# Passages between sublayers: five products ahead of the norm and three with it, squares added on VectorE, G units packed toward the middle of a stage

## Chip, core and metric

The kernel runs on one core of a Trainium2 chip. The metric is the device time of one execution in microseconds (us); of several runs the median counts.

## The reference, cut to what matters

Two transformer blocks run over T = 256 tokens of width D = 1024, all in fp32. The change touches the six sublayers of the first block; the second block (short convolution, two expert layers, differential attention) is untouched.

```python
def rmsnorm(x, g):
    y = x * lax.rsqrt(jnp.mean(x * x, axis=-1, keepdims=True) + EPS)
    return y * g

def swiglu(h, w_gu, w_down):                 # w_gu: 1024 x 5632, w_down: 2816 x 1024
    gate, up = jnp.split(h @ w_gu, 2, axis=-1)
    return (jax.nn.silu(gate) * up) @ w_down

def sublayer(x, shift, scale, gate, g_pre, g_post, fn, res_weight):
    h = rmsnorm(x, g_pre) * (1 + scale[:, None, :]) + shift[:, None, :]
    return x + res_weight * gate[:, None, :] * rmsnorm(fn(h), g_post)
...
mods = jnp.split(c_act @ cond_w[layer] + cond_b[layer], 9, axis=-1)   # shift, scale, gate of each sublayer
```

Each of the two layers runs three sublayers: an FFN (`swiglu`), a mixer (GLA, gated linear attention, in the first layer; MLA, latent attention, in the second) and another FFN.

## The kernel before

**Weights.** Every fp32 product is three matmuls in a reduced form of fp32 (hi x hi, hi x lo, lo x hi; lines 297 to 299, and 320 to 323 in the passages). So each weight passes through a split. It comes as a unit of 128 x 1024 (512 KB): SP issues its DMA into a raw buffer, ACT casts it to the high half (L237), DVE subtracts for the low half (L248). The products of the conditioning vector `c` with `cond_w` and the like are not matmuls: such a "G unit" is one DVE instruction over a raw buffer (L251), which the profile shows with a second row that reads the sum out. `build_plan` writes one list of all units, W and G, and its `mix` deals a stage's G units evenly between the W units that follow the first `LEAD`. Raw buffers are a ring of four, with one or two more during an FFN; there are eight slots for split pairs. `next_w` is called where a weight is used: it splits everything up to that weight, then `prefetch(n_ahead)` splits up to three units more, if their slots are free.

**Order.** Each engine runs its instructions in the order of the code. A DVE instruction that is written behind a split cannot start before that split, and a split not before its DMA and its cast.

**An FFN.** 22 row blocks f. For each, the `gu` product gives the gate and the up part in one bank; ACT takes SiLU (L677), DVE multiplies (L678), ACT casts the product to its high half (L345), DVE subtracts for its low half `tL` (L348; called `a` for the first 14). `out_proj` then multiplies by `w_down` into `y`, which needs all 22. As each `y` block ends, ACT squares it (L557) and DVE adds the squares (L560); `pst` sums them over the channels on PE.

**A passage.** Between two sublayers PE would stand still while x is updated and its norm taken. So the first products of the next sublayer are computed before its norm is known: `ahead` updates x block by block (L604, L607), scales it (L471, L462), multiplies it by the weights of four output blocks (`first`, 258 columns wide for two extra terms), and sums x's squares with eight products `st` (L351). `scaled_rstd` takes the root on ACT and the reciprocal on DVE (L622 to L625), `apply` normalises x (L434, L435, L428) for four more products (`second`), and the `first` products are scaled afterwards (`late`). x stays scaled by an unknown factor `x_r`; the next update multiplies by it (L599), and before the convolution `unscale` (L614) divides it out, during the last FFN. There are five such passages: to GLA, to the second FFN, to the third FFN (with the products of MLA's keys and values, "kv"), to MLA, and to the fourth FFN.

In time, the four FFNs lie at about 55 to 225, 376 to 571, 572 to 784 and 888 to 1085 us, GLA and MLA between them.

## Time and profile before

| | |
|---|---|
| median of 3 runs | 2981.62 us (2979.09 to 2990.97) |
| profiled execution | 2977.33 us, span 2975.4 us |
| mean granted clock of TensorE | 0.985 of full speed |
| PE, DVE, ACT busy | 95%, 81%, 49% of the span |
| DMA | 630.43 MB, mean 212 GB/s |

The engines are PE (TensorE, matmuls), PEld (its weight loads), DVE (VectorE), ACT (ScalarE), POOL and SP (which issues the DMAs). "L248" is line 248 of the kernel. `out<-in` names the tiles written and read. A row of a timeline has start, duration, engine, line, operation, tiles and shapes; what stands in brackets at its end is how long its engine sat idle before it and which instruction ended that. A row of the waits says which engine and line waited for which, the total, the number and the longest. PEclk is the granted clock of TensorE, 1.00 for 2.4 GHz and 0.50 for 1.2.

### The profile page before, as it was taken

What the parts mean: (1) busy time and instruction counts of PE and PEld (TensorE: products, weight loads), DVE (VectorE), ACT (ScalarE), POOL (GpSimd) and SP (SyncE); (2) the same over time, 40 slices, a digit from 0 to 9 for tenths busy, and PEclk for the clock granted to TensorE, in tenths of its full rate; (3) what the DMA queues carried; (4) which work ended last, traced back from release to release, by engine and by line L of the source; (5) the groups of instructions that cost most, each with busy time, mean ns of one, the idle gap of its engine ahead of it and who ended that gap; (6) DMA issues with size and microseconds to landing.
All of it is one profiled execution on the core that took longest, in us unless ns stands there. A gap on an engine that the chain in (4) does not pass through costs nothing.

```text
span 2975.4 us, 60705 instructions
## 1 busy us (share of the span) xinstructions
PE 2831.2 (95%) x24914; PEld 2764.5 (93%) x24914; DVE 2399.3 (81%) x4373; ACT 1465.7 (49%) x2140; POOL 6.8 (0%) x16
## 2 busy tenths in 40 slices
PE   6998999999999999999999999989799999999998
PEld 5997889999879999999999999988799999999998
DVE  6978689687768978998997887767689988788754
ACT  4555555455555545545444444446554544444543
POOL 0000000000000000000000000000000000000000
PEclk8999999999999999999999999999999999999999
DMA  7995569578636966465556557874245655655662
GB/s 270 360 327 181 185 225 335 203 282 302 213 128 247 335 211 229 144 190 178 178 193 221 176 178 250 300 254 142 98 131 187 190 172 190 215 177 177 221 191 93
DMA packets 173174, 630.43 MB, mean 212 GB/s; under 512 B 19319, under 2 KB 20343, under 8 KB 172768
## 3 DMA queue, kind: packets, MB, share of 16 engines
q1 hardware_dynamic: 172080, 623.98, 62.8%
q8 instruction: 195, 3.19, 0.4%
q0 software_dynamic: 816, 2.57, 0.3%
q14 instruction: 83, 0.68, 0.1%
HBM read 625.43 MB, written 1.05 MB: 211 GB/s over the span
## 4 chain that ended last, share of the span: by engine, by line
PE 71%; DVE 12%; DMA 10%; ACT 5%; issue 2%; SPq 0%; ACTq 0%; DVEq 0%
PE u L297 7%; PE u L299 7%; PE u L298 7%; PE ya L297 6%; PE ya L298 6%; PE ya L299 6%; PE gu L299 3%; PE gu L298 3%; PE gu L297 3%; DVE xl L248 2%; DMA raw<-in_peer_v_dram 2%; PE y L298 2%; PE y L299 2%; PE y L297 2%; DVE wl L248 2%
## 5 line engine op out<-in xcount | busy, mean ns | idle before, releaser
L237 ACT CAST wh<-raw 128x1024 fp32r<-128x1024 f32 x535 | 559.7, 1048 | 573.5 <-PE ya L298 228.4
L248 DVE TENSOR_TENSOR wl<-raw,wh 128x1024 fp32r<-128x1024 f32 x535 | 653.2, 1224 | 165.4 <-ACT wh L237 163.1
L297 PE MATMUL u<-hH,wh 128*128 128x256 f32 x2048 | 575.3, 281 | 0.0
L299 PE MATMUL u<-hH,wl 128*128 128x256 f32 x2048 | 570.1, 278 | 2.0 <-DVE wl L248 1.9
L298 PE MATMUL u<-hL,wh 128*128 128x256 f32 x2048 | 569.1, 278 | 0.0
L298 PE MATMUL ya<-hL,wh 128*128 128x256 f32 x1424 | 395.3, 278 | 8.3 <-DVE hL L348 8.3
L297 PE MATMUL ya<-hH,wh 128*128 128x256 f32 x1424 | 400.0, 281 | 2.6 <-ACT hH L345 2.6
L299 PE MATMUL ya<-hH,wl 128*128 128x256 f32 x1424 | 394.4, 277 | 0.0
L299 PEld LDWEIGHTS u<-hH,wl 128*128 128x128 f32 x2048 | 386.7, 189 | 3.5 <-DVE wl L248 3.1
L298 PEld LDWEIGHTS u<-hL,wh 128*128 128x128 f32 x2048 | 385.6, 188 | 0.0
L297 PEld LDWEIGHTS u<-hH,wh 128*128 128x128 f32 x2048 | 384.6, 188 | 0.0
L248 DVE TENSOR_TENSOR xl<-raw,xh 128x1024 fp32r<-128x1024 f32 x235 | 286.1, 1222 | 94.9 <-ACT xh L237 93.8
L237 ACT CAST xh<-raw 128x1024 fp32r<-128x1024 f32 x235 | 244.8, 1049 | 237.5 <-DMA raw<-in_ffn_gu_dram 49.4
L298 PEld LDWEIGHTS ya<-hL,wh 128*128 128x128 f32 x1424 | 268.3, 188 | 9.7 <-DVE hL L348 9.7
L297 PEld LDWEIGHTS ya<-hH,wh 128*128 128x128 f32 x1424 | 268.2, 188 | 3.2 <-ACT hH L345 3.2
L299 PEld LDWEIGHTS ya<-hH,wl 128*128 128x128 f32 x1424 | 268.5, 189 | 0.0
L299 PE MATMUL gu<-hH,xl 128*128 128x256 f32 x744 | 208.3, 280 | 4.8 <-DVE xl L248 4.8
L298 PE MATMUL gu<-hL,xh 128*128 128x256 f32 x744 | 208.1, 280 | 0.0
L297 PE MATMUL gu<-hH,xh 128*128 128x256 f32 x744 | 208.0, 280 | 0.0
L298 PE MATMUL ya<-hL,xh 128*128 128x256 f32 x624 | 174.7, 280 | 10.1 <-DVE hL L348 10.0
L297 PE MATMUL ya<-hH,xh 128*128 128x256 f32 x624 | 175.2, 281 | 0.5 <-ACT hH L345 0.4
L299 PE MATMUL ya<-hH,xl 128*128 128x256 f32 x624 | 172.9, 277 | 0.0
(566 smaller groups left out, 7278.6 us busy)
## 6 DMA issues: line engine op xcount, KB each, us to landing
raw<-in_peer_u_dram SPq DMA_DIRECT2D x256, 512.0 KB, 3.7
raw<-in_peer_v_dram SPq DMA_DIRECT2D x234, 512.0 KB, 3.8
raw<-in_ffn_gu_dram SPq DMA_DIRECT2D x107, 512.0 KB, 5.1
raw<-in_cond_w_dram SPq DMA_DIRECT2D x92, 512.0 KB, 4.9
raw<-in_ada_w_dram SPq DMA_DIRECT2D x71, 512.0 KB, 4.6
raw<-in_ffn_down_dram SPq DMA_DIRECT2D x57, 512.0 KB, 5.0
fix<-in_ffn_gu_dram SPq DMA_DIRECT2D x53, 512.0 KB, 5.2
fix<-in_cond_w_dram SPq DMA_DIRECT2D x43, 512.0 KB, 5.1
```

Of the source, the lines that this page charges most:

```text
L237: self.nc.scalar.copy(self.slots[self.slot[n]][0], self.raw[n])
L248: nc.vector.tensor_tensor(wl, raw, wh.bitcast(F32), op=OP.subtract)
L297: mm(out, lhsT=wh, rhs=xh, start=start, stop=False, **kw)
L298: mm(out, lhsT=wh, rhs=xl, start=False, stop=False, **kw)
L299: mm(out, lhsT=wl, rhs=xh, start=False, stop=stop, **kw)
```

## The change

- In the passages to GLA and to the second and fourth FFN, `ahead` takes five products and `apply` three; the passage to the third FFN keeps four and four, that to MLA its three.
- Where there are more than three products ahead, DVE adds the squares of seven blocks one to another as they come, and PE sums two operands in place of eight; the products of k = 5 stand ahead of the sums.
- `scaled_rstd` is called before `prefetch`, which takes two units and not three; the one behind `apply` takes one and not two.
- The reciprocal of `x_r` moves from `apply` into `unscale`, and x is unscaled in every sublayer, block by block between other work.
- In `out_proj`, over the last 24 row blocks, splits run up to five units ahead, and two at the last unit.
- `LEAD` goes from 9 to 11, and with `TAIL` the last five W units of a stage come without G units.

```diff
--- before.py
+++ after.py
@@ -39,12 +39,12 @@
 
 SCRATCH = 8192
 
-AHEAD, AHEAD_MLA, AHEAD_PEER = 3, 2, 2
+AHEAD, AHEAD_END, AHEAD_MLA, AHEAD_PEER = 3, 5, 2, 2
 
 N_START = 6
 
 CUTS = (56, 76, 112, 150, 154, 194, 200, 248, 248)
-LEAD, LEAD_CONV, LEAD_U, LEAD_V, LEAD_ATTN = 9, 24, 100, 74, 12
+LEAD, TAIL, LEAD_CONV, LEAD_U, LEAD_V, LEAD_ATTN = 11, 5, 24, 100, 74, 12
 N_U = 10
 
 
@@ -437,8 +437,7 @@
                 low(d - 1)
         low(KO - 1)
         self.hold = False
-        nc.vector.reciprocal(self.x_r, self.x_r)
-        self.prefetch(2)
+        self.prefetch(1)
 
     def ahead(self, A, S, n):
 
@@ -452,15 +451,19 @@
         s2 = S.unsqueeze(2).to_broadcast([128, KO, 2])
         nc.scalar.copy(tH[:, :, T:T + 2], s2)
         nc.vector.tensor_tensor(tL[:, :, T:T + 2], s2, tH[:, :, T:T + 2].bitcast(F32), op=OP.subtract)
-        outs = [self.bank("y", "first") for _ in range(n)]
+        outs = [self.bank(b, "first") for b in "yyyym"[:n]]
         cols = [o[:, 0:T + 2] for o in outs]
         ws = self.open_group(n)
         st = self.bank("x", "st")[:, :T]
         sq = self.yg
 
+        n_add = KO - 1 if n > 3 else 1
+
         def low(d):
             nc.vector.scalar_tensor_tensor(tL[:, d, 0:T], x[:, d], A[:, d:d + 1], tH[:, d, 0:T].bitcast(F32),
                                            op0=OP.mult, op1=OP.subtract)
+            if 0 < d < n_add:
+                nc.vector.tensor_tensor(sq[:, 0], sq[:, 0], sq[:, d], op=OP.add)
             if d < 5:
                 self.k_mm(cols, ws, ht, d)
 
@@ -475,12 +478,16 @@
             if d:
                 low(d - 1)
         low(KO - 1)
-        for d in range(KO):
-            self.sums(st, sq[:, d], d == 0, d == KO - 1)
-        self.prefetch(3, True)
-        for k in range(5, KO):
+        if n > 3:
+            self.k_mm(cols, ws, ht, 5)
+        self.sums(st, sq[:, 0], True, False)
+        for d in range(n_add, KO):
+            self.sums(st, sq[:, d], False, d == KO - 1)
+        r = self.scaled_rstd(st)
+        self.prefetch(2, True)
+        for k in range(6 if n > 3 else 5, KO):
             self.k_mm(cols, ws, ht, k)
-        return outs, self.scaled_rstd(st)
+        return outs, r
 
     def ahead_ln(self, m, stats, n):
 
@@ -571,8 +578,12 @@
             y = self.bank("m" if lead and d < lead + 2 else "y", "y")[:, :T]
             for k in range(KB):
                 if n % 8 == 0:
-                    self.hold = n + 8 >= KB * (KO - lead)
+                    left = KB * (KO - lead) - n
+                    if left <= 24:
+                        self.n_ahead = AHEAD_END if left > 8 else 2
                     cur = self.next_w()
+                    self.n_ahead = AHEAD
+                    self.hold = left <= 8
                 s = slice(n % 8 * 128, n % 8 * 128 + 128)
                 self.mm3(y, cur[0][:, s], cur[1][:, s], aH[k], aL[k], k == 0, k == KB - 1)
                 n += 1
@@ -592,16 +603,14 @@
     def scaled_update(self):
 
         nc = self.nc
-        q = s = self.t("rstd")
+        s = self.t("rstd")
         nc.scalar.activation(s, self.post_st, AF.Sqrt, scale=1.0 / D, bias=self.cst(C_E6))
-        if self.x_scaled:
-            q = self.t("rstd")
-            nc.vector.tensor_tensor(q, s, self.x_r, op=OP.mult)
+        assert not self.x_scaled
         us = {}
 
         def one(d):
             t = us[d] = self.t("u")
-            nc.vector.tensor_tensor(t, self.x[:, d], q, op=OP.mult)
+            nc.vector.tensor_tensor(t, self.x[:, d], s, op=OP.mult)
 
         def two(d):
             nc.vector.tensor_tensor(self.x[:, d], us.pop(d), self.yg[:, d], op=OP.add)
@@ -610,6 +619,8 @@
     def unscale(self):
 
         self.x_scaled = False
+        self.nc.vector.reciprocal(self.x_r, self.x_r)
+        yield
         for d in range(KO):
             self.nc.vector.tensor_tensor(self.x[:, d], self.x[:, d], self.x_r, op=OP.mult)
             yield
@@ -679,27 +690,40 @@
             self.split_later(*a[f], sg)
 
         f = 0
-        for g, u in zip(early[::2], early[1::2]):
-            if r is None:
-                finish(f, g, u)
-            else:
+        plain = []
+        n_e = len(early) if r is not None else 0
+        both = list(early) + list(second)
+        for i in range(0, len(both), 2):
+            g, u = both[i:i + 2]
+            if i + 1 < n_e:
                 sg = self.t("sg")
                 z, b = self.late(g, r)
                 nc.scalar.activation(sg, z, AF.Silu, bias=b)
                 z, b = self.late(u, r)
                 nc.vector.scalar_tensor_tensor(sg, z, b, sg, op0=OP.add, op1=OP.mult)
                 self.split_later(*a[f], sg)
+            elif i < n_e:
+                sg = self.t("sg")
+                z, b = self.late(g, r)
+                nc.scalar.activation(sg, z, AF.Silu, bias=b)
+                nc.vector.tensor_tensor(sg, sg, u, op=OP.mult)
+                self.split_later(*a[f], sg)
+            else:
+                finish(f, g, u)
             f += 1
-        for g, u in zip(second[::2], second[1::2]):
-            finish(f, g, u)
-            f += 1
+        n_f = f
         for f in range(f, FB):
-            ps = self.bank("y", "gu")
+            ps = self.bank("x" if r is not None and f == n_f else "y", "gu")
             for o in (ps[:, :T], ps[:, T:]):
                 self.unit_mm(o, *self.h)
             finish(f, ps[:, :T], ps[:, T:])
             if todo and f in todo:
                 todo[f]()
+            if self.x_scaled or plain:
+                if f == n_f + 2:
+                    plain.append(self.unscale())
+                if plain and f > n_f + 1:
+                    next(plain[0], None)
         self.out_proj([i for i, _ in a], [i for _, i in a], gate(), during=during)
         self.close("ffn")
 
...
@@ -846,11 +871,13 @@
                 self.unit_mm(ps[:, :T], hH, hL)
                 nc.scalar.copy(k[:, i % 4], ps[:, :T])
                 step()
+                next(plain)
             ready["qk"] = True
             vp = [self.bank("y", "vp") for _ in range(4)]
             for kk in range(8):
                 self.v_unit(vp, kk, hH, hL)
                 step()
+                next(plain)
             for i in range(4):
                 nc.scalar.copy(v[:, i // 2, i % 2 * 512:i % 2 * 512 + 512], vp[i])
             ready["v"] = True
...
@@ -1746,12 +1776,12 @@
                 a = a[i]
             return [("W", a[j], any_, RAW if any_ else RAW_FEW) for j in range(a.shape[0])]
 
-        def mix(w, g, lead):
-
-            n, m = len(w) - lead, len(g)
+        def mix(w, g, lead, tail=0):
+
+            n, m = len(w) - lead - tail, len(g)
             out, j = w[:lead], 0
             for i, u in enumerate(w[lead:]):
-                while j < m and j * n <= i * m:
+                while j < m and j * n <= i * m and i < max(n, 1):
                     out.append(g[j])
                     j += 1
                 out.append(u)
@@ -1772,7 +1802,7 @@
                 plan.extend(g[:14] + w[:1] + g[14:16] + w[1:2])
                 g, w = g[16:], w[2:]
             n = len(plan)
-            mix(w, g, LEAD)
+            mix(w, g, LEAD, TAIL)
             if more:
                 k = n + (len(plan) - n) * 6 // 10
                 plan[n + 15:k] = using(RAW + more, plan[n + 15:k])
@@ -1828,21 +1858,21 @@
             return self.ahead(m[:, 8:16], m[:, 0:8], n)
 
         def second(m, r, n=4):
-            outs = self.halves(n)
+            outs = self.halves(n, "mm" if n == 4 else "mx")
             self.apply(r, m[:, 8:16], m[:, 0:8], outs)
             return outs
 
         self.gla_loads()
         m = self.mod_pre(0, 1)
-        first, r = rms(m, 4)
+        first, r = rms(m, 5)
         self.acts("natural_log_exp_and_others")
-        outs = second(m, r)
+        outs = second(m, r, 3)
         self.gla(lambda: self.mod_gate(m, 0, 1), first, outs, r)
 
         m = self.mod_pre(0, 2)
-        first, r = rms(m, 4)
+        first, r = rms(m, 5)
         self.acts("silu_and_others")
-        outs = second(m, r)
+        outs = second(m, r, 3)
         self.load_c("c_2", self.c2)
         tables = self.rope_tables()
         todo = {f: lambda: next(tables, None) for f in range(9, 18)}
@@ -1865,12 +1895,10 @@
         self.mla(lambda: self.mod_gate(m, 1, 1), first, r)
 
         m = self.mod_pre(1, 2)
-        first, r = rms(m, 4)
+        first, r = rms(m, 5)
         self.acts("silu_and_others")
-        outs = second(m, r)
-        plain = self.unscale()
-        todo = {f: lambda: next(plain, None) for f in range(8, 17)}
-        self.ffn(lambda: self.mod_gate(m, 1, 2), first, outs, r, todo)
+        outs = second(m, r, 3)
+        self.ffn(lambda: self.mod_gate(m, 1, 2), first, outs, r)
 
         m, st = self.conv(self.ada_cols(0, 0), lambda: self.ada_cols(0, 1, 0))
         m, st = self.peer(0, m, st, lambda: self.ada_cols(1, 0, 1))
```

On DVE at the end of the first FFN's `gu` part the rows before are these. L248 is a W unit, L251 a G unit, the last row `tL` of f = 21.

```order
L248 TENSOR_TENSOR wl_81<-raw_88,wh_80 128x1024
L251 SCALAR_TENSOR_TENSOR raw_f,mods<-raw_f,fix 128x1024
L348 TENSOR_TENSOR tL<-fix,tH 128x256
L248 TENSOR_TENSOR wl_83<-fix,wh_82 128x1024
L678 TENSOR_TENSOR fix<-fix,gu 128x256
L657 TENSOR_TENSOR mod<-mods,vt 128x8
L658 SCALAR_TENSOR_TENSOR mod<-mod,vt 128x8
L248 TENSOR_TENSOR wl_85<-raw_86,wh_84 128x1024
L251 SCALAR_TENSOR_TENSOR raw_87,mods<-raw_87,fix 128x1024
L348 TENSOR_TENSOR tL<-fix,tH 128x256
```

With the change the same place reads so (L678 is L689 now):

```order
L248 TENSOR_TENSOR wl_81<-fix,wh_80 128x1024
L251 SCALAR_TENSOR_TENSOR raw_86,mods<-raw_86,fix 128x1024
L348 TENSOR_TENSOR tL<-fix,tH 128x256
L248 TENSOR_TENSOR wl_83<-raw_87,wh_82 128x1024
L251 SCALAR_TENSOR_TENSOR raw_88,mods<-raw_88,fix 128x1024
L689 TENSOR_TENSOR fix<-fix,gu 128x256
L668 TENSOR_TENSOR mod<-mods,vt 128x8
L669 SCALAR_TENSOR_TENSOR mod<-mod,vt 128x8
L248 TENSOR_TENSOR wl_85<-raw_f,wh_84 128x1024
L251 SCALAR_TENSOR_TENSOR fix,mods<-fix 128x1024
L348 TENSOR_TENSOR tL<-fix,tH 128x256
```

One G unit more (L251 behind the split of `wl_83`) stands between the low half of f = 20 and that of f = 21.

On DVE at the end of `ahead` in the first passage, before (L622 and L624 are the sum and the reciprocal of `scaled_rstd`, L434 the first instruction of `apply`):

```order
L462 SCALAR_TENSOR_TENSOR tL<-x,mod,tH 128x256 x2
L248 TENSOR_TENSOR xl_105<-raw_86,xh_104 128x1024
L248 TENSOR_TENSOR wl_81<-raw_87,wh_80 128x1024
L248 TENSOR_TENSOR wl_83<-raw_88,wh_82 128x1024
L622 TENSOR_TENSOR fix<-fix,st 128x256
L624 RECIPROCAL fix<-fix 128x256
L434 SCALAR_TENSOR_TENSOR fix<-x,mod,fix 128x256 x2
```

And now, with L633, L635 and L466, the addition of squares:

```order
L463 SCALAR_TENSOR_TENSOR tL<-x,mod,tH 128x256
L466 TENSOR_TENSOR fix<-fix 128x256
L463 SCALAR_TENSOR_TENSOR tL<-x,mod,tH 128x256
L633 TENSOR_TENSOR fix<-fix,st 128x256
L635 RECIPROCAL fix<-fix 128x256
L248 TENSOR_TENSOR wl_81<-raw_87,wh_80 128x1024
L248 TENSOR_TENSOR wl_83<-raw_88,wh_82 128x1024
L434 SCALAR_TENSOR_TENSOR fix<-x,mod,fix 128x256 x2
```

Three splits stood ahead of L622; now two stand between the reciprocal and L434.

On ACT at the end of GLA's `out_proj`, before the second passage (L557 squares a block, L237 is a cast, L453 begins the passage):

```order
L557 ACTIVATE fix<-y 128x256
L558 ACTIVATE fix<-y,mod 128x256
L237 CAST wh_80<-raw_87 128x1024
L557 ACTIVATE fix<-y 128x256
L558 ACTIVATE fix<-y,mod 128x256
L557 ACTIVATE fix<-y 128x256
L558 ACTIVATE fix<-y,mod 128x256
L453 CAST tH<-mod 128x8x2
```

And now (L557 is L564, L453 is L452):

```order
L237 CAST wh_80<-raw_87 128x1024
L564 ACTIVATE fix<-y 128x256
L565 ACTIVATE fix<-y,mod 128x256
L237 CAST wh_82<-raw_88 128x1024
L564 ACTIVATE fix<-y 128x256
L565 ACTIVATE fix<-y,mod 128x256
L452 CAST tH<-mod 128x8x2
```

One cast, of `wh_82`, has come in ahead of the last square.

## Rows read from the trace of the kernel before

**Rows 1.** The page: busy time of the engines, and the chain's shares.

```profile
PE 2831.2 (95%) x24914; PEld 2764.5 (93%) x24914; DVE 2399.3 (81%) x4373; ACT 1465.7 (49%) x2140; POOL 6.8 (0%) x16
...
PE 71%; DVE 12%; DMA 10%; ACT 5%; issue 2%; SPq 0%; ACTq 0%; DVEq 0%
```

**Rows 2.** PE's waits over the span: us in total, times, longest us.

```profile
PE first L320 <- ACT tH L471: 12.0, 5, 2.5
...
PE gu L299 <- DVE xl L248: 4.8, 2, 2.5
...
PE vp L901 <- DVE xl L248: 3.9, 1, 3.9
...
PE y L298 <- DVE tL L348: 3.0, 2, 2.0
```

**Rows 3.** A stretch: us; PE, PEld, DVE, ACT, POOL busy; PEclk; DMA share; GB/s.

```profile
100.00:125.00 25.00, 25.00 (x223) 25.00 (x222) 23.64 (x36) 13.95 (x20) 0.00 (x0) 1.00 1.00 378
```

**Rows 4.** ACT's waits from 640 to 670, in the third FFN.

```profile
ACT xh L237 <- DMA raw<-in_ffn_gu_dram: 7.9, 4, 2.6
```

**Rows 5.** First and third FFN, L248 alone, then L251: us; DVE busy (x).

```profile
72.30:168.72 96.42, 44.07 (x37) 1.00 0.97 354
609.00:728.41 119.41, 54.41 (x45) 1.00 0.91 321
...
72.30:168.72 96.42, 34.29 (x55) 1.00 0.97 354
609.00:728.41 119.41, 34.35 (x56) 1.00 0.91 321
```

**Rows 6.** Timeline of DVE: the last low half in each FFN.

```profile
168.72 0.42 DVE L348 TENSOR_TENSOR tL<-fix,tH 128x256 fp32r<-128x256 f32 x1
...
513.57 0.42 DVE L348 TENSOR_TENSOR tL<-fix,tH 128x256 fp32r<-128x256 f32 x1
...
728.41 0.42 DVE L348 TENSOR_TENSOR tL<-fix,tH 128x256 fp32r<-128x256 f32 x1
...
1028.68 0.42 DVE L348 TENSOR_TENSOR tL<-fix,tH 128x256 fp32r<-128x256 f32 x1
```

**Rows 7.** Timeline of PE: first `y` of each FFN, and the `y` that waited.

```profile
159.64 0.28 PE L297 MATMUL y<-a,xh 128*128 128x256 f32 x1
...
169.19 0.39 PE L298 MATMUL y<-tL,xh 128*128 128x256 f32 x1 [2.04 <-DVE tL L348]
...
509.47 0.28 PE L297 MATMUL y<-a,xh 128*128 128x256 f32 x1
...
718.41 0.28 PE L297 MATMUL y<-a,xh 128*128 128x256 f32 x1
...
1022.17 0.28 PE L297 MATMUL y<-a,xh 128*128 128x256 f32 x1
```

**Rows 8.** First passage: group of the sums, then timelines of DVE and PE.

```profile
L351 PE MATMUL st<-fix,cs 128*128 128x256 f32 x16 | 3.6, 379 | 0.0
...
234.79 2.35 DVE L248 TENSOR_TENSOR wl<-raw,wh 128x1024 fp32r<-128x1024 f32 x2
237.15 0.42 DVE L622 TENSOR_TENSOR fix<-fix,st 128x256 f32<-128x256 f32 x1
238.15 1.75 DVE L624 RECIPROCAL fix<-fix 128x256 f32<-128x256 f32 x1 [0.58 <-ACT fix L623]
...
241.20 0.28 PE L320 MATMUL second<-hH,xh 128*128 128x256 f32 x1
```

**Rows 9.** Timeline of ACT, second passage: one of the casts before the squares.

```profile
370.74 1.05 ACT L237 CAST xh<-raw 128x1024 fp32r<-128x1024 f32 x1 [1.17 <-DMA raw<-in_ffn_gu_dram]
```

**Rows 10.** Stretches with PEclk, columns as in rows 3.

```profile
170.00:200.00 30.00, 30.00 (x263) 30.00 (x262) 24.30 (x32) 13.79 (x19) 0.00 (x0) 1.00 0.92 337
250.00:275.00 25.00, 21.07 (x107) 17.09 (x107) 16.86 (x32) 13.69 (x24) 0.00 (x0) 0.86 0.57 206
365.00:412.00 47.00, 41.08 (x314) 39.15 (x313) 38.87 (x77) 29.59 (x57) 0.54 (x1) 0.96 0.38 128
```

More of the change, by code (lines that the diff above doesn't have):

```diff
@@ L710, in halves @@
             if i % 2 == 0:
-                b = self.bank(which, "second")
+                b = self.bank(which[i // 2 % len(which)], "second")
             r.append(b[:, i % 2 * T:i % 2 * T + T])
@@ L749, in gla @@
             for i in range(3):
+                nc.scalar.copy(k[:, i], second[i])
+            for i in (3, 0, 1, 2):
                 self.late_to(q[:, i], early[1 + i], rs)
-            for i, ps in enumerate(second):
-                nc.scalar.copy((q[:, 3], k[:, 0], k[:, 1], k[:, 2])[i], ps)
+            plain = self.unscale()
             def core():
@@ L1048, in mla @@
             self.kv_heads(norm)
-            nc.vector.reciprocal(self.x_r, self.x_r)
+            plain = self.unscale()
+            next(plain)
             self.n_ahead = AHEAD
@@ L1107, in mla @@
                         nc.scalar.copy(qn[:, m - 9:m - 7], ps)
+                if m < 8:
+                    next(plain)
                 if m >= 10:
```

## Prediction

> **What bounds the kernel now.** I read the page first. PE is busy 95% of the span, and the chain that ended last is PE for 71%, DVE for 12% and DMA for 10% [rows 1]. So the matmuls set the time, and a change can win or lose only where PE stands waiting or has matmuls less. The list of PE's waits says where that is [rows 2]: 12.0 us in five waits at the start of a passage (line 320 after the cast L471), 3.0 us at the first down product of an FFN (`y` after the low half `tL`, L348), 4.8 us in two waits of an FFN's `gu` product for a weight's low half, and one of 3.9 us in the GLA sublayer. None is long, so the change has little to take away there.
>
> The second view is the table by stretches. In the `gu` part of an FFN, PE is busy without a break, DVE is busy 23.64 of 25 us, and the DMA engines run at a share of 1.00 and move 378 GB/s [rows 3]. In the same part ACT waits for weights that are still in flight, 7.9 us in four waits within 30 us [rows 4]. There the **supply of units** (512 KB each, one DMA and one DVE instruction L248 or L251) sets when DVE comes to an instruction that stands behind them. Its pace: from 72.30 to 168.72 DVE ran 37 rows of L248 and 55 of L251, and as each G unit shows two rows there (one reads its sum) these are some 64 units, 96.42 / 64 = 1.51 us each. The same from 609 to 728.41: 45 + 28 units, 119.41 / 73 = 1.64 us [rows 5]. For the second and the fourth FFN I take 1.51, the lower of the two.
>
> What waits for DVE there is the last low half of the activation, `tL` of f = 21. It stands in DVE's program behind all the splits and G units that the plan put ahead of it. It starts at 168.72, 513.57, 728.41 and 1028.68 in the four FFNs [rows 6], while PE is through with `gu` at 159.64, 509.47, 718.41 and 1022.17, where its first `y` starts [rows 7]. So the lags are 9.1, 4.1, 10.0 and 6.5 us. PE can cover some of it with the other 21 row blocks of `y`: at a lag of 9.1 it waited 2.04 us at 169.19 [rows 7], so about 7.1 us are covered. Two FFNs have no cover left, the fourth has 0.6 us, the second 3.0 us.
>
> **The change, part by part.**
>
> *The plan (LEAD 9 to 11, TAIL 5).* Two more weight units lead each stage, and the last five have no G units. The same G units are packed more densely between, and so more of them come ahead of f = 21. I counted the rows L248 and L251 of DVE's order from the tenth `gu` unit on: three units more in the first three FFNs and four in the last (the first pair of excerpts shows the end of the first FFN: every split there now has a G unit behind it). At the pace above they cost 3 x 1.51 = 4.5, again 4.5, 3 x 1.64 = 4.9 and 4 x 1.51 = 6.0 us of lateness. Less the cover, PE waits 4.5, 1.5, 4.9 and 5.4 us more, 16.3 in all. The freer end of the stage gives back little, since PE's waits [rows 2] name nothing of that part that is long. The lead could at best be filled by two units in advance of need, which would take 3 us from each: the bottom is 16.3 - 12, some 4.
>
> A page of the Trainium skill bears on the pace: DMA: Bandwidth & Descriptors, section Where 436 GB/s comes from, puts the limit of one core from HBM at about 358 GB/s, which is 1.46 us for 512 KB, and so 13 x 1.46 = 19 us of lateness in place of 20. The trace has a stretch at 378 GB/s [rows 3], over that limit.
>
> *x unscaled in mid sublayer.* Eight multiplications go into every sublayer where x was left scaled till the end; the last FFN has them already. At the 0.42 us of the addition L622, on a tile of the same size [rows 8], they are 3.4 us. The reciprocal is only moved, from `apply` (L440) to behind it, and in the FFNs both places lie ahead of f = 21: nothing. In the second and third FFN the 3.4 us stand ahead of f = 21 too. Where DVE has pauses they are free, where splits follow each other they are all lateness: 0 to 3.4. I take 1.5 each, nearer the lower end, because ACT's waits [rows 4] are pauses of DVE too: 3.0. In return one multiplication of 0.43 us (L599, of the size of L622) goes from ahead of x's update in four passages: -1.7.
>
> *Five products ahead, three behind.* The number of products does not change (eight), the order does. The eight products of squares become two in four passages. They are 16 rows of 3.6 us [rows 8], so six of them, 12 rows, are 2.7 us of PE. The added additions on DVE cost 0.42 us each and lie beside x's update, whose chain through ACT sets the pace of DVE there, about 1.1 us for each d; six of them fill its pauses and push the end by perhaps 0.6 us.
>
> *The root ahead of two splits, and the cover behind it.* Before, the sums end at 237.15 (L622 starts), the root and the reciprocal L624 follow, and `second` starts at 241.20 without a pause of PE [rows 8], for three groups of `first` (k = 5 to 7, 36 matmuls) stand between. Now the code's order has the two splits (2.35 us as one row of two [rows 8]) between the reciprocal and L434 (second pair of excerpts). So `second` comes 4.05 + 2.35 = 6.4 us after the sums, while only k = 6 and 7 cover it: 30 matmuls at 0.118 us (36 of them fill the 4.25 us from 237.0 to 241.2), 3.5 us. PE waits 2.9 us, 3.6 in the passage to kv, which has four products ahead and not five (24 matmuls, 2.8), against 2.7 saved by the squares. Three of those come out at 0.2 each, kv at 0.9. The MLA passage saves no squares; its cover is 27 matmuls, 3.2 us, its wait 0.8 before by the same reckoning and 3.2 after: 2.4. The splits themselves come no earlier in DVE's program than before, so weights due behind them gain nothing. Bounds: if something else ahead of L434 already delays it, 0 to -2.7 each; at the most the wait lets the clock fall, below.
>
> *Casts at the end of out_proj.* AHEAD_END sends one cast more ahead of the last square on ACT (third pair). The cast before it shows what it brings, 1.05 us and a wait for its DMA of 1.17 [rows 9]: 2.2 us in the passage after GLA, where `first` cannot start until the squares are summed; elsewhere the unit is there already, 0. In GLA itself the unscaling (3.4) lies ahead of the `vp` wait of 3.9 us [rows 2] and one G unit less (1.2 us) lies there too: I take half, 1.1.
>
> Sum: plan 16.3, unscaling in FFNs 3.0, passages 0.6 + 0.9 + 2.4 - 1.7, cast 2.2, GLA 1.1: **+24.8**. Some waits then take the place of others: the two waits of `gu` for a low half (4.8 us) [rows 2] come just behind the new waits of `second` and vanish, for PE arrives later. That leaves +20.0. The profiled execution took 2977.33 us, so 2997.3, rounded 2997. The profiled one lies 4.3 under the median of the runs, 2981.62; against that 2997 is +0.5%. A measurement of this kernel tells about 0.5% (15 us) from no change: faster is under 2966.7, slower over 2996.5. The likeliest case alone runs from 2985 to 3009.
>
> **The clock.** PE runs at 2.4 GHz nearly everywhere, and after the wait of 3.9 us in GLA the stretch 250 to 275 shows 0.86, that is 1.2 GHz for 28% of it and 3.5 us lost; after the wait of 2.5 us at the start of the second passage the stretch of 47 us shows 0.96, 1.9 us lost [rows 10]. So each new wait over 3 us may lose another 2 to 3.5 us. In the sum it stands at nothing.
> The Trainium skill, TensorE: Matmul & The Clock Gate, section HAM oscillation, says that pauses between batches of matmuls send the clock back to half each time; by it each of the six new waits would cost as the one in GLA, 21 us. The trace is not so strict: at 169.19 PE waited 2.04 us [rows 7], and the stretch from 170 to 200 shows 1.00 [rows 10].
>
> **Rivals.**
> - *The lead pays* (no change). The two weights in advance and the pauses of DVE take up the denser G units, the waits for `tL` stay at 2 us and none, and only the passages and the cast remain: about +6, 2983. For it: DVE has pauses, 1.4 us in 25 [rows 3]. Against: the DMA share of 1.00 there, and raws that come free only with a split.
> - *The passages pay* (faster, the other side). The squares' 10.8 us leave PE, no wait comes before `second` because DVE reaches the splits while ACT's root still runs, the four multiplications take 1.7, and the half clock at the passages goes with shorter starts, four times 1.9: 2977.3 - 20.1 = 2957.2. It decides at `second`: if it starts within 4.3 us of the sums. Against: reciprocal, splits and L434 stand on one engine in order.
> - *The clock falls at the new waits* (slower still). Four waits over 3.9 us at `y` and some at `second`, each 3.5 more: 2997 + 4 x 3.5 = 3011. For it the 0.86 [rows 10], against it the 2.04 us that cost nothing.
>
> **How the numbers follow.** My forecast has 0.42, the lead pays 0.27, the passages pay 0.17, the clock falls 0.14. The forecast lies at the edge of what can be told, but its unknowns (a falling clock, DVE's pauses filled) reach further up than down: of its chance I put 0.13 under 2996.5. So faster 0.17, same 0.27 + 0.13 = 0.40, slower 0.29 + 0.14 = 0.43. The range 2962 to 3013 leaves out most of the faster rival and the top of the clock's.
>
> **What would show it.** Right: in the waits of PE, `y` after `tL` L348 rises from 3.0 us to 15 or more, with `tL` 4 to 7 us later behind the end of `gu`; a new wait of `second` after `hH` of 2 to 4 us in four passages; the sums with 2 products. Wrong: `second` starting without a wait, `tL` with its lags of before, or DMA shares of the `gu` parts clearly under 0.95, which would mean that the supply was not the bound.

## The result and the profile after

The changed kernel takes 3035.92 us (median of 4 runs, 3033.76 to 3042.26) against 2980.36 for the kernel before on the same chip. The medians lie 55.6 us apart; the ratio that the experiments go by (an estimate from the runs, not the quotient of the medians) is 1.0165 with a 95% interval of 1.0142 to 1.0189, that is 49 us, 42 to 56. The direction was forecast, the size was not: 2997 was predicted, and the range ended at 3013. The profiled execution took 3037.9 us with a span of 3036.1, 60.7 more than before.

The waits of PE, over the span (us in total, times, longest):

```profile
PE y L297 <- ACT tH L345: 17.3, 6, 4.3
PE second L320 <- ACT hH L435: 10.6, 4, 3.2
PE y L298 <- DVE tL L348: 10.3, 7, 2.1
...
PE upd L833 <- ACT gla L882: 7.1, 1, 7.1
...
PE gu L299 <- DVE xl L248: 4.2, 2, 3.3
```

Against [rows 2], `y` waits 27.6 us in place of 4.6 (3.0 for `tL` and 1.6 for `tH`). The larger part, 17.3 us, is now for the cast `tH` (L345), and `tL` has 10.3, where the prediction looked for 15 or more. `second` waits where it did not, and GLA's `upd` has a wait of 7.1 us that is new. The wait of `gu` for a low half, which the prediction let vanish, has stayed (4.8 to 4.2).

The last low half of each FFN on DVE, and the first `y` on PE, as in [rows 6, 7]:

```profile
173.45 0.42 DVE L348 TENSOR_TENSOR tL<-fix,tH 128x256 fp32r<-128x256 f32 x1
...
548.86 0.42 DVE L348 TENSOR_TENSOR tL<-fix,tH 128x256 fp32r<-128x256 f32 x1
...
769.09 0.42 DVE L348 TENSOR_TENSOR tL<-fix,tH 128x256 fp32r<-128x256 f32 x1
...
1086.21 0.42 DVE L348 TENSOR_TENSOR tL<-fix,tH 128x256 fp32r<-128x256 f32 x1
```

```profile
163.36 0.28 PE L297 MATMUL y<-a,xh 128*128 128x256 f32 x1
...
532.81 0.28 PE L297 MATMUL y<-a,xh 128*128 128x256 f32 x1
...
750.18 0.38 PE L297 MATMUL y<-a,xh 128*128 128x256 f32 x1 [0.28 <-DVE fix L689]
...
1070.75 0.28 PE L297 MATMUL y<-a,xh 128*128 128x256 f32 x1
```

The lags are 10.1, 16.1, 18.9 and 15.5 us; they were 9.1, 4.1, 10.0 and 6.5. In three FFNs DVE comes 9 to 12 us later behind the end of `gu`, in the first 1.0. Part of this is PE coming earlier, as e2 shows below.

The first passage on DVE, in its timeline (the part behind the last scaling of x):

```profile
239.76 0.47 DVE L463 SCALAR_TENSOR_TENSOR tL<-x,mod,tH 128x256 fp32r<-128x256 f32 x1
244.42 0.42 DVE L633 TENSOR_TENSOR fix<-fix,st 128x256 f32<-128x256 f32 x1 [4.19 <-PE st L351]
245.42 1.75 DVE L635 RECIPROCAL fix<-fix 128x256 f32<-128x256 f32 x1 [0.58 <-ACT fix L634]
247.09 2.29 DVE L248 TENSOR_TENSOR wl<-raw,wh 128x1024 fp32r<-128x1024 f32 x2
249.30 0.88 DVE L434 SCALAR_TENSOR_TENSOR fix<-x,mod,fix 128x256 f32<-128x256 f32 x2
```

In [rows 8] three splits filled the time until the sums were there, and L622 followed the last of them at once. Now DVE stands idle for 4.19 us, and the two splits come behind the reciprocal, so `second` waits on PE:

```profile
250.38 0.38 PE L320 MATMUL second<-hH,xh 128*128 128x256 f32 x1 [2.46 <-ACT hH L435]
```

Over the five passages DVE's wait for the sums grew:

```profile
DVE fix L633 <- PE st L351: 18.4, 5, 4.8
```

Before, the same view said

```profile
DVE fix L622 <- PE st L351: 5.7, 3, 2.7
```

By stretches between first uses of the same tiles, the span's growth lies in the down products of the last three FFNs (first `y` to the next passage or convolution: 64.8 to 76.1, 69.2 to 80.2 and 66.7 to 77.2 us, +33), in GLA (first `second` to first `y`: 119.9 to 130.3), and in the five passages with what leads into them. The `gu` parts of the last three FFNs (first `second` to first `y`) are 2.8, 2.5 and 2.1 us shorter.

### The profile page after: what moved, and what is told of

The parts are those of the page before. It is cut to its first block, busy times and chain, and to the rows that moved or that the text cites. A ratio compares the mean times of both kernels' runs of the same rounds, so it can differ in the third digit from the quotient of the medians.

```text
span 3036.1 us, 60703 instructions
## 1 busy us (share of the span) xinstructions
PE 2849.5 (94%) x24866; PEld 2778.1 (92%) x24866; DVE 2416.5 (80%) x4431; ACT 1466.6 (48%) x2140; POOL 6.8 (0%) x16
## 4 chain that ended last, share of the span: by engine, by line
PE 66%; DVE 13%; DMA 13%; ACT 5%; issue 3%; SPq 0%; ACTq 0%; DVEq 0%
PE u L297 7%; PE u L299 7%; PE u L298 7%; PE ya L297 6%; PE ya L298 6%; PE ya L299 6%; DMA raw<-in_peer_v_dram 3%; DVE xl L248 3%; DVE wl L248 3%; DMA raw<-in_ffn_gu_dram 2%; PE y L298 2%; PE y L299 2%; PE y L297 2%; DMA fix<-in_ffn_gu_dram 2%; ACT xh L237 1%
## 5 line engine op out<-in xcount | busy, mean ns | idle before, releaser
L237 ACT CAST wh<-raw 128x1024 fp32r<-128x1024 f32 x534 | 558.7, 1048 | 581.1 <-PE ya L298 229.4
L248 DVE TENSOR_TENSOR wl<-raw,wh 128x1024 fp32r<-128x1024 f32 x534 | 648.9, 1218 | 167.1 <-ACT wh L237 165.1
L237 ACT CAST xh<-raw 128x1024 fp32r<-128x1024 f32 x241 | 251.3, 1049 | 262.1 <-DMA raw<-in_peer_v_dram 57.8
L248 DVE TENSOR_TENSOR xl<-raw,xh 128x1024 fp32r<-128x1024 f32 x241 | 292.8, 1221 | 102.9 <-ACT xh L237 102.0
```

Of the source, the lines that this page charges most:

```text
L237: self.nc.scalar.copy(self.slots[self.slot[n]][0], self.raw[n])
L248: nc.vector.tensor_tensor(wl, raw, wh.bitcast(F32), op=OP.subtract)
```

## The experiments

All ratios are to the kernel before, run on the same chip between the others; brackets are 95% intervals. Executions of one kernel spread over some 20 us here, so costs are taken from ratios, and traces only say where.

**Which part.** Four edits of one part each; the plan was also put alone onto the kernel before.

```diff
-LEAD, TAIL, LEAD_CONV, LEAD_U, LEAD_V, LEAD_ATTN = 11, 5, 24, 100, 74, 12
+LEAD, TAIL, LEAD_CONV, LEAD_U, LEAD_V, LEAD_ATTN = 9, 0, 24, 100, 74, 12
```

> The changed kernel with LEAD 9 and TAIL 0 again, all else as changed. Theory P (the denser G units are the cause: they come ahead of the last low half in the FFNs, PE waits at the first down product and the clock falls behind the wait): the waits of y for tH/tL of 27.6 us fall under 8, the stretch from the first y to the next passage is again 65 to 70 us in the last three FFNs, GLA loses most of its 10 us, time 2990 to 3000 us. Theory U (the unscaling of x on DVE is the cause): the waits at y stay above 18 us, time 3020 to 3030. Theory Q (the passages, with the root ahead of two splits, are the cause): waits at y stay, time 3025 to 3036.

Measured: 1.0089 [1.0052, 1.0126], 3017.5 us, so 0.76% or 22 us are the plan's (by the two intervals between 10 and 36); waits at `y` fell to 14.7 us. Less came back than theory P said, so the plan is the largest single part that was found and not the only one.

> The kernel before with LEAD 11 and TAIL 5 alone. Theory P: waits at y rise from 4.6 us to some 20, with half clock behind them, and time is 3010 to 3025 us. Theories U and Q: within 10 us of before, 2975 to 2992.

Measured: 1.0101 [1.0068, 1.0134]. On the kernel before, where nothing else was changed, `y` waits 30.9 us:

```profile
PE y L297 <- ACT tH L345: 19.7, 7, 4.8
...
PE y L298 <- DVE tL L348: 11.2, 8, 1.9
...
PE upd L808 <- ACT gla L855: 5.3, 1, 5.3
```

The wait in GLA comes with the plan too; without it (e1) it is 1.1 us. GLA's 20 G units stood between 24 of its 33 W units and stand between 17 now; that this is the reason was not tried.

Not all of the wait at `y` is DVE's doing. In the second FFN, `second` starts at 394.16 before:

```profile
394.16 0.28 PE L320 MATMUL second<-hH,xh 128*128 128x256 f32 x1
```

and with the plan alone

```profile
411.95 0.28 PE L320 MATMUL second<-hH,xh 128*128 128x256 f32 x1
...
521.76 0.28 PE L297 MATMUL y<-a,xh 128*128 128x256 f32 x1
...
535.89 0.42 DVE L348 TENSOR_TENSOR tL<-fix,tH 128x256 fp32r<-128x256 f32 x1
```

From `second` to the last low half DVE took 119.4 us [rows 6] and takes 123.9, so it comes 4.5 us later. From `second` to the first `y` PE took 115.3 [rows 7] and takes 109.8: it comes 5.5 us earlier. The third and fourth FFN say the same (DVE 4.4 and 4.2 later, PE 5.0 and 5.9 earlier); in the first DVE comes 5.0 us later and PE as before. PE is earlier because its matmuls run at the faster of the two paces of the last section, and because it waits less for weights in `gu` (1.6 us in place of 7.6). What PE waits at `y` because it came earlier costs nothing. So the plan's price is read from whole FFNs: from the start or from `second` to the next passage they take 6.8, 3.3, 7.0 and 6.0 us more, 23 in all, and GLA 6.8.

```diff
-        r = self.scaled_rstd(st)
         self.prefetch(2, True)
+        r = self.scaled_rstd(st)
```

> The changed kernel with the two splits ahead of the root again (prefetch, then scaled_rstd). Theories P and U: the four waits of second for hH (10.6 us) go, with the short falls of the clock behind them, 10 to 15 us less: 3021 to 3026 us. Theory Q: DVE comes earlier to all that follows, waits at y fall too, 2995 to 3010.

Measured: 1.0123 [1.0091, 1.0154], 0.42% or 12 us less (1 to 24 by the intervals). The waits of `second` fell from 10.6 to 2.4 us and DVE's wait for the sums from 18.4 to 7.8, but those at `y` stayed at 31.5. Theories P and U had this number. By the timelines the time lies in the passages themselves: from the first `first` to the first product behind `second`, the four passages other than MLA's take 117.4 us in the changed kernel and 105.5 here, 11.9 less, while the last three FFNs' down products take 231.6 in place of 233.5.

```diff
...
+        self.n_un += 1
+        self.nc.vector.reciprocal(self.x_r, self.x_r)
+        if self.n_un < 5:
+            yield
+            for d in range(KO):
+                yield
+            return
         self.x_scaled = False
-        self.nc.vector.reciprocal(self.x_r, self.x_r)
...
```

> The changed kernel without the 32 multiplications in GLA, MLA and two FFNs; x stays scaled until the last FFN and the four multiplications ahead of x's update are back; the reciprocal stays where the change put it. Theory U: 3.4 us of DVE less ahead of y in two FFNs and in GLA, so with the clock 20 to 30 us less, 3005 to 3015. Theory P: 2 x 3.4 us less waiting at most, 3027 to 3034.

Measured: 1.0170 [1.0141, 1.0200], as the change itself. Theory U falls: in the whole change the 32 multiplications cost nothing that can be told (the difference is +1 us, -10 to +13).

**Is it the clock?** By the trace's records of the granted clock, the half clock rose from 61 us to 140 in the first 1250 us. The matmuls added here write a bank that nothing reads.

```diff
+                if d == 0 and KB == 22 and k >= 20 and self.n_split > 150:
+                    fill = self.bank("x", "fill")[:, :T]
+                    for _ in range(24):
+                        self.nc.tensor.matmul(fill, lhsT=cur[0][:, s], rhs=aH[0], start=True, stop=True)
```

> The changed kernel with 24 matmuls into an unread bank ahead of each of the last two row blocks of the first y in the last three FFNs: 2 x 24 x 0.113 = 5.4 us of PE work in each where PE waited 6 to 9 us. Theory C (most of the time goes to the half clock that follows the waits, not to the waits): the half clock of 10 us behind each of the three waits goes, 3 x 5 = 15 us less than the changed kernel, 3018 to 3025 us. Rival W (the waits themselves are the cost, the clock comes back at once): no change, 3033 to 3040.

Measured: 1.0180 [1.0155, 1.0204]. The table by stretches (us; PE, PEld, DVE, ACT, POOL busy; PEclk; DMA share; GB/s), at the three first `y` of the changed kernel:

```profile
533.00:557.00 24.00, 15.99 (x107) 15.09 (x106) 20.29 (x32) 13.07 (x18) 0.00 (x0) 0.79 0.92 325
750.00:775.00 25.00, 14.65 (x94) 13.45 (x95) 20.13 (x30) 12.03 (x16) 0.00 (x0) 0.80 0.83 276
1070.00:1094.00 24.00, 16.49 (x118) 15.79 (x117) 20.17 (x31) 12.86 (x18) 0.00 (x0) 0.79 0.96 342
```

and with the waits filled:

```profile
533.00:559.00 26.00, 23.21 (x197) 22.61 (x197) 20.95 (x33) 13.46 (x18) 0.00 (x0) 1.00 0.90 303
752.00:777.00 25.00, 20.66 (x151) 19.96 (x150) 18.05 (x28) 11.36 (x15) 0.00 (x0) 0.86 0.84 272
1070.00:1094.00 24.00, 20.30 (x171) 19.70 (x171) 21.17 (x31) 12.29 (x17) 0.00 (x0) 1.00 0.95 327
```

The clock stays up in two of the three and is better in the third (0.79, 0.80, 0.79 to 1.00, 0.86, 1.00), and the time doesn't follow: the three stretches to the next passage shrink by 2.8, 1.4 and 0.7 us. Half of the half clock falls into time in which PE waits anyway: in the changed kernel's three stretches it lasts 33.0 us, and PE is busy in 17.0 of them. Theory C falls: the 15 us that it forecast would have shown (the difference to the change is +4 us, -6 to +15), though a gain of some 5 us, as in the stretches, is not excluded. Of some 11 us per FFN the waits are the larger share.

This was tried at the three `y` alone. In GLA the clock fell too, before

```profile
295.00:330.00 35.00, 33.56 (x217) 27.15 (x215) 24.96 (x38) 18.40 (x34) 0.00 (x0) 1.00 0.67 224
```

and after

```profile
295.00:330.00 35.00, 23.27 (x101) 19.63 (x102) 26.35 (x41) 15.10 (x22) 0.00 (x0) 0.66 0.89 295
```

and in e5 it stands at 0.73 there. By the same records, from GLA's first `second` to its first `y` PE worked 30.1 us at half clock, against 15.8 before. At full clock half of the difference would go, so the clock can be up to 7 us of GLA's 10; this is an estimate, and holding the clock up there was not tried. Over the first 1250 us the same reckoning gives at most 27 us (95.7 against 42.3), of which e5 tried 7 (81.4).

**The rest.** With both repairs:

> The changed kernel with LEAD 9 and TAIL 0 and with the two splits ahead of the root: what is left is five and three products, the squares on DVE, the unscaling and AHEAD_END. If plan and order add up (20 and 11 us): 3002 to 3010 us. If the rest by itself is harmless: 2982 to 2992. Waits of second for hH under 3 us, waits at y under 12 us.

Measured: 1.0066 [1.0044, 1.0089]: plan and order add up, and 20 us remain (13 to 27).

```diff
-AHEAD, AHEAD_END, AHEAD_MLA, AHEAD_PEER = 3, 5, 2, 2
+AHEAD, AHEAD_END, AHEAD_MLA, AHEAD_PEER = 3, 3, 2, 2
```

> As e6_plan_and_splits, with AHEAD_END 3 in place of 5 at the end of out_proj. If the cast ahead of the last squares costs the 2.2 us of the prediction in several passages: 3 to 8 us less than e6; if not, equal within 3 us.

Measured: 1.0051 [1.0030, 1.0072], not to be told from e6.

Then the parts on the kernel before: e10 has the five and three products with the squares on DVE, e9 the same with `prefetch(2, True)` and `prefetch(1)` in place of 3 and 2, e11 the unscaling.

> As e9, with three and two units split at the passage as before: the five and three products and the squares on DVE alone. If the squares pay as the prediction priced them (2.7 us in four passages): 2974 to 2981 us. If DVE's six additions and the shorter cover give it back: 2983 to 2992.

Measured: 1.0009 [0.9989, 1.0029], no gain and no loss, 3 us (-3 to +9). By the prediction's own terms it should have been 8 us less: 10.8 for the squares, and 2.8 back for waits of `second` with the splits ahead. Those waits came (2.4 us), the gain did not. The sums are shorter, but with five products more matmuls stand ahead of them: in the second passage they start 13.6 us behind the first `first`, before 8.9. The four passages of e3 take 110.1 us in e10 and 109.8 before; in e13 and e14, which add other parts to these, 105.5 and 107.9, so little of the gain is seen at best.

> The kernel before with five and three products, the squares on DVE and the splits ahead of the root, two and one units at the passage as in the change; no unscaling, no AHEAD_END, old plan. Theory N (the number of units split at the passage counts: what is not split there comes later, onto DVE's full stretch): 2992 to 3002 us, and 8 us or more over e10. Theory X (the unscaling is what remains of the 20 us in e6): 2975 to 2990, as e10.

Measured: 1.0065 [1.0045, 1.0085]. This loss has its own place, though. Three weights are needed at `second`, and with no unit split early at the end of `out_proj` the third is now split behind the reciprocal, after a wait for its cast (DVE, first passage):

```profile
244.47 1.75 DVE L632 RECIPROCAL fix<-fix 128x256 f32<-128x256 f32 x1 [0.58 <-ACT fix L631]
247.19 1.23 DVE L248 TENSOR_TENSOR wl<-raw,wh 128x1024 fp32r<-128x1024 f32 x1 [0.97 <-ACT wh L237]
248.34 0.88 DVE L434 SCALAR_TENSOR_TENSOR fix<-x,mod,fix 128x256 f32<-128x256 f32 x2
```

`second` waits 9.8 us in e9 and 2.4 in e6 and e10, so e9 shows that two units need those early splits (with AHEAD_END 3, in e8, `second` waits 3.5), and does not explain e6.

> The kernel before with the unscaling in mid sublayer alone (reciprocal and eight multiplications in GLA, MLA and each FFN, no multiplication ahead of x's update). Theory X: waits at y rise by 8 us or more and time is 2995 to 3008. Theory N: within 6 us of before, as in e4_x_left_scaled, where taking the multiplications out changed nothing.

Measured: 1.0012 [0.9998, 1.0027]: by itself no loss that can be told.

Next, e6 with the counts restored (e13), then without AHEAD_END too (e14), and e6 without the unscaling (e16):

```diff
-        self.prefetch(1)
+        self.prefetch(2)
...
-        self.prefetch(2, True)
+        self.prefetch(3, True)
```

> As e6_plan_and_splits (1.0066 of before), with three and two units split at the passage and not two and one. Theory N (fewer units split there are what remains): 1.000 to 1.003 of before. Theory X (the unscaling together with AHEAD_END): 1.005 to 1.008, as e6.

Measured: 1.0017 [1.0000, 1.0034]. `prefetch` 3 and 2 in place of 2 and 1 takes 0.49%, some 15 us (6 to 23).

```diff
-                    left = KB * (KO - lead) - n
-                    if left <= 24:
-                        self.n_ahead = AHEAD_END if left > 8 else 2
+                    self.hold = n + 8 >= KB * (KO - lead)
                     cur = self.next_w()
-                    self.n_ahead = AHEAD
-                    self.hold = left <= 8
```

> As e13, without AHEAD_END: e10 with the unscaling added. Theory N: 1.000 to 1.003. Theory X with the unscaling as the part that counts: 1.004 to 1.008; if AHEAD_END counts, 0.003 under e13.

Measured: 1.0010 [0.9993, 1.0028]; AHEAD_END counts for nothing that can be told.

```diff
-            if self.x_scaled or plain:
-                if f == n_f + 2:
-                    plain.append(self.unscale())
-                if plain and f > n_f + 1:
-                    next(plain[0], None)
...
+            q = self.t("rstd")
+            nc.vector.tensor_tensor(q, s, self.x_r, op=OP.mult)
...
```

> As e6, with x left scaled (no unscaling in mid sublayer, reciprocal in apply again): five and three products, AHEAD_END, two and one units. Theory N: 1.004 to 1.008, as e6. Theory X: 1.000 to 1.003.

Measured: 1.0025 [1.0005, 1.0044], against theory N: e6 lies 12 us higher (3 to 21). So with fewer units split *and* the unscaling 15 to 20 us are lost (e8, e6), with the one or the other alone 3 to 8. Neither theory had that. It is not firm, though: e6 has four runs, e8 is not clear of e16, and in the whole change, which has both, leaving x scaled gave nothing back (e4).

Nor does a trace show where this time goes. The wait of ACT's casts for `gu` weights in flight that differs most is 60.6 us in e6 and 43.6 in e13:

```profile
ACT xh L237 <- DMA raw<-in_ffn_gu_dram: 60.6, 39, 3.7
```

But in e16, which is near e13 in time, it is 53.1, and all rows of such waits together (first 1250 us) come to 145.0 us in e6, 134.4 in e13 and 141.0 in e16, which does not go with the times. That the counts act through raw buffers that come free later is a guess; it was not tried.

**The opposite of the plan.** If G units ahead of `y` set the time, moving them toward the end must gain. On the kernel before, with `late` 3, 2 and 1:

```diff
-                while j < m and j * n <= i * m:
+                while j < m and (j * n <= i * m if not late else j * n * n <= i * m * (n - (n - i) // late)):
...
-            mix(w, g, LEAD)
+            mix(w, g, LEAD, 3)
```

> The kernel before with the G units of the six stages moved toward the end of each stage, 2 to 3 units less ahead of the last low half of an FFN, the opposite of the change. Theory P: waits at y fall from 4.6 us to under 2, those of gu for a low half from 7.6 to about 5, time 5 to 10 us less than before. If the pace of the units is not what counts there: within 3 us of before.

Measured: 0.9987 [0.9973, 1.0002], no gain that can be told.

> As e7 (0.9987 of before), with the G units moved further toward the end, 3 to 4 units less than before ahead of the last low half. Theory P: 0.996 to 0.999 of before. If down products now wait for weights: over 1.001.

Measured: 0.9954 [0.9933, 0.9975], 2975.93 against 2989.06: 13 us faster than the kernel before (7 to 20 by the interval), and the fastest of all. That later G units are faster is shown; that the waits at `y` are the reason is not. They fell by 1.2 us only, to 3.4, and the four FFNs are 4.6 us shorter in the traces; where the rest lies, one trace of each does not tell. The sums behind the down products begin to wait (5.8 us; 2.4 before), most of it here:

```profile
PE pst L351 <- DVE fix L560: 3.6, 2, 2.4
```

> As e15, with the G units later still, 7 to 8 units less than before ahead of the last low half. Near the end of a stage each W unit has more than one G unit beside it, some 3.4 us of supply for 2.8 us of PE, so down products, squares and pst wait: 1.000 to 1.010 of before. If the supply there has room: under e15, 0.990 to 0.995.

Measured: 1.0017 [0.9998, 1.0036]; the wait has moved to the end of the stage:

```profile
PE pst L351 <- DVE fix L560: 14.1, 5, 5.1
```

e12 puts the plan of e7 onto e10, e17 that of e15 onto e13.

> e10 with the G units moved toward the end of each stage as in e7. If both gains hold: 2968 to 2978 us, under both kernels. If the waits at y were hidden already: as e10.

Measured: 1.0019 [0.9997, 1.0041], no gain.

> As e13 (five and three products, unscaling, AHEAD_END, with the order and counts of before), with the G units as late as in e15. If the supply ahead of y was what hid the squares' gain: 0.990 to 0.996 of before, under e15. If the parts of the change are worth nothing in themselves: 0.995 to 1.000.

Measured: 0.9991 [0.9972, 1.0009]; 11 us above e15 (3 to 19): the change's other parts take back what the later plan gives.

## Why the prediction was wrong

The way was forecast, the size was not: +20 predicted, 49 measured (42 to 56). Three terms of the sum failed: the squares' gain of 10.8 us, which did not come; the plan's price in GLA, put at a small gain; and the counts of units split at a passage, put at nothing. The other terms were nearly met or are small.

- *The bound* was right: the supply of units sets when DVE comes to the last low half. e2 shows it: there DVE comes 5.0, 4.5, 4.4 and 4.2 us later in the four FFNs, and the prediction had 4.5, 4.5, 4.9 and 6.0. Its count of units was high by three (the traces have 3, 2, 2 and 3 more G units ahead of the last low half, not 3, 3, 3 and 4), and its pace of 1.5 us a unit was low (18.1 us for these 10 units, 1.8 each); the two errors nearly cancel, by luck.
- *The plan: 16.3 us predicted, 22 to 30 measured* (e1, e2; the intervals reach from 10 to 40). In the FFNs it cost 23 (e2), somewhat more than forecast. That the waits at `y` were nearly met (4.6 + 16.3 + 3.0 = 23.9 predicted, 27.6 measured) is in part luck: FFN by FFN 4.5, 3.0, 6.4 and 5.4 more were predicted, and 0.6, 8.0, 7.0 and 7.5 came, since the prediction took the end of `gu` as fixed and PE moved it. What the term left out is GLA, priced at the unscaling less one G unit (1.1 us): it lost 10, of which 7 came with the plan (6.8 in e2, and 7.3 went in e1).
- *The order of root and splits* was priced rightly and then set off against a gain that was not there. Its waits of `second` and in the MLA passage were put at 14.7 us; e3, which takes 12 of these back by the same reckoning, measured 12 (1 to 24). For `second` in four passages 12.3 were predicted, 10.6 came.
- *The squares: 10.8 us of gain predicted* against those waits, to leave 3.9 for the passages. e10 shows no gain (-3 to +9 us where -8 was due). PE has less to sum, but five products put more matmuls ahead of the sums, so `second` comes no earlier.
- *The counts: nothing predicted, some 15 us measured* (e6 against e13, 6 to 23). The prediction spoke of two splits behind the reciprocal and never asked where the third, and the second behind `apply`, went. The loss shows together with the unscaling only (e16), and its mechanism stays open.
- *The unscaling: 3.0 + 1.1 - 1.7 predicted*, nothing that can be told alone (e11) and in the whole change (e4), some 12 us with the counts (e6 against e16). The sum added its terms as if each had its cover to itself; e6, e13 and e16 speak against that, e4 does not.
- *The cast, 2.2:* not to be told (e8, e14). *The vanishing of `gu`'s waits, -4.8:* wrong, 4.2 us stayed.
- *The clock* stood at nothing, with 3.5 us a wait as a rival. It fell behind the long waits, to 0.79 and 0.80 at the three `y` and to 0.66 in GLA. The Trainium skill (TensorE: Matmul & The Clock Gate, section HAM oscillation) says that pauses between batches of matmuls send the clock back to half; the trace agrees at these four places. That it costs as much as the rival had it, e5 does not bear out at `y`; for GLA it stays open.
- The rival with the lead that pays is refuted by e2, the one in which the passages pay by the waits of `second`.

## What to carry to other kernels

Price an order by the cover that is left: two splits of 2.35 us put into the short chain from the sums to `second` cost 12 us in five passages, as reckoned (e3). A gain in one engine's work is a gain in time only if what waits for it comes earlier: the squares saved PE matmuls and `second` no time (e10). Count for every prefetch how many units it does less, not only where it stands (e13). Read a change's price from whole stretches and not from one wait, since a wait grows also when the engine that waits arrives earlier (e2). And an even spread of side work is not the best by itself: e15 is faster with it later, up to the point where the end of the stage fills (e18).

## What was not expected of the hardware

Behind the waits the clock fell to 1.2 GHz for a time: the granted clock was 0.66 in GLA (295 to 330 us) and 0.79 at `y`, where it had been 1.00 before. Yet with the waits at `y` filled and the clock at 1.00 in two of three places and 0.86 in the third, the time did not change beyond its interval (e5). A granted clock is therefore no price by itself: how long PE works under it has to be counted.

The matmuls have two paces at full clock. Before, [rows 3] count 223 in 25 us, 0.112 us each, and the same product in the second FFN 257 in 30 us, 0.117 each:

```profile
440.00:470.00 30.00, 30.00 (x257) 30.00 (x256) 29.25 (x51) 17.96 (x27) 0.00 (x0) 1.00 0.98 353
```

After, it is the other way round: the first FFN has the slower pace, the second the faster. What sets it was not tried. These are two stretches of the changed kernel:

```profile
100.00:130.00 30.00, 30.00 (x257) 30.00 (x256) 27.82 (x43) 14.83 (x21) 0.00 (x0) 1.00 1.00 373
...
450.00:480.00 30.00, 30.00 (x267) 30.00 (x266) 26.57 (x42) 15.32 (x23) 0.00 (x0) 1.00 0.93 328
```

With the plan alone (e2), the second FFN has the faster pace too. The same stretch, before and in e2:

```profile
480.00:505.00 25.00, 25.00 (x215) 25.00 (x213) 23.53 (x40) 12.91 (x20) 0.00 (x0) 1.00 0.91 317
```

```profile
480.00:505.00 25.00, 25.00 (x223) 25.00 (x223) 24.68 (x44) 12.51 (x19) 0.00 (x0) 1.00 0.86 311
```

In the first FFN, where DVE sets the end, the faster pace gives nothing. Up to its last 24 row blocks this FFN is the same code in all kernels with one plan. With the plan of before, the last low half lags the first `y` by 8.4 to 10.3 us in the seven traces in which this FFN has the faster pace (most of its matmuls start 113 ns apart), and by 4.9 to 5.9 in the three with the slower (118 ns); with the plan of the change by 14.0 to 14.6 in three and by 10.1 and 10.9 in two. At 4% of 100 us PE comes 4 us earlier and waits 4 us longer: up to the next passage the first FFN takes 224.9 to 229.4 us at the faster pace and 227.0 to 229.9 at the slower (plan of before).
